# An encoder trunk's opening norm: one product spreads the sums, ScalarE seeds the inverse root, and a low part is issued ahead of a dot product

## The chip, the cores and the metric

The kernel runs on one core of a Trainium2 chip. The metric is the device time of one execution in microseconds (us), as the median of several runs. The core has a matrix engine (TensorE, "PE" in the profile, with its weight loads shown as "PEld"), a vector engine (VectorE, "DVE"), an activation engine (ScalarE, "ACT"), a general engine (GpSimd, "POOL") and a queue that issues most of the transfers (SyncE, "SP"). Each engine takes its instructions in the order in which they stand in its own program.

## The reference

Two layers, each made of a gated feed-forward half step, a mixer of three branches, and a second feed-forward half step. Every sub-layer starts with a norm that is shifted and scaled by values computed from a conditioning vector `c`. The change touches only the first norm of the first layer and what is multiplied with it:

```
def rms_norm(x, gain):
    xf = x.astype(jnp.float32)
    y = xf * lax.rsqrt(jnp.mean(xf * xf, axis=-1, keepdims=True) + EPS)
    return (y * gain.astype(jnp.float32)).astype(x.dtype)

def modulate(h, shift, scale):
    return h * (1 + scale[:, None, :]) + shift[:, None, :]

c_act = jax.nn.silu(c)
mod = (c_act @ w_ada[l] + b_ada[l]).reshape(B, N_MOD, D_MODEL)
h = modulate(rms_norm(x, norm_gain[l, 0]), mod[:, 0], mod[:, 1])
... swiglu(h, ffn_w_gate[l, 0], ffn_w_up[l, 0], ffn_w_down[l, 0])
```

There are 512 tokens of 1024 values. `mod[:, 0]` is the shift and `mod[:, 1]` the scale: 1024 values each, and each of them is a dot product of 1024 weights with `c_act`.

## The kernel before

**Layout.** Activations lie transposed: the 1024 features stand on 128 partitions in 8 blocks (`d` = 0 to 7), and the 512 tokens along the free axis. Every product is computed as three products: each operand is split into a high part in a narrower format and a low part (what the high part leaves over), and `triple` (lines 117 to 122) issues high x high, high x low and low x high. For a block of `h` these parts are `hhi` and `hlo`, for weights `whi` and `wlo`.

**The opening** is the method `start` of `Ffn`. x arrives in four transfers, ACT squares its eight blocks, and DVE adds the squares up (`ssum`, lines 693 and 695). The sum over the 128 partitions is made on PE: four products with one column of ones (line 699) give the sums of 4 x 128 tokens as a 128x4 tile. On that small tile DVE computes 1/sqrt with an integer first guess and three Newton steps (lines 299 to 308). To bring the result back along the free axis, DVE and ACT build four diagonal blocks (lines 708 and 710), and one product with a tile of ones (line 713) spreads them into `rb`, a 128x512 tile that holds 1/rms for every token on every partition.

**Then come the 8 blocks d.** For each one:

- two *dot products* on DVE (line 206, `mod_step`/`mod_dot`): the shift, written (0,d) below, and the scale, (1,d). Each reads a 128x1024 tile of `w_ada` that SP loads into one of four buffers with the tag "v2". The four are taken in turn, in the order (0,0), (1,0), (0,1), (1,1), ..., so that the load of a tile can be issued only when the dot product four places earlier in that order has been done;
- ACT makes the scale column `apre` from (1,d) (line 213);
- DVE multiplies x by `rb` (line 722, the tile `t`; two buffers);
- ACT writes `hhi` from `t` with scale and shift (line 724), and a second time in full precision into a PSUM tile (line 726);
- DVE writes `hlo` as the difference (line 727, "the low part");
- a 128x768 chunk of weights (`w_first`) is loaded into one of two raw buffers, ACT casts it to `whi`, GpSimd writes `wlo` (lines 290 and 292);
- PE issues 18 matmuls of 128x512 (3 gate and 3 up tiles, three products each).

**What sets the order.** A scheduler lays out the program of each engine. `tc.issue_after(x)` and `behind(engine)` only tell it that an instruction is to stand behind another one in the program. SP's transfers stand in the order (0,d), (1,d), chunk d, (0,d+1), and so on; a transfer that waits for its buffer holds up all that stand behind it. After the 8 blocks PE goes on with the gate and up products of the next weight tiles (`unit`, whose first weights are the pair `self.early`), and DVE with the remaining dot products (`mod_queue`), weight splits and block sums for later (line 490).

Of the kernel before, what the change touches and what calls it, by code (L numbers as in the profile page):

```python
# [15 lines left out]
F32 = mybir.dt.float32  # L16
F32R = mybir.dt.float32r
I32 = mybir.dt.int32
AF = mybir.ActivationFunctionType
ALU = mybir.AluOpType  # L20
AX = mybir.AxisListType

P = 128
T = 512
D = 1024
KD = D // P
# [5 lines left out]
NT = T // P  # L32
EPS = 1e-6
# [7 lines left out]
def encoder_kernel(tc, xT, c, w_ada, b_ada, gains, w_gate, w_up, w_down, w_qkv, w_f, w_ubg,  # L41
                   qk_gain, rel, fbias, w_pool, pool_scale, w_branch, w_out, inv_cnt, w_first, out):
    nc = tc.nc
    pools = []

    def open_pool(**kw):
        p = tc.tile_pool(**kw)
        pools.append(p)
        return p.__enter__()

    cp = open_pool(name="consts", bufs=1)
# [4 lines left out]
    mm = nc.tensor.matmul  # L56
# [3 lines left out]
    def nm(s):  # L60
        uid[0] += 1
        return f"{s}_{uid[0]}"

    def st(shape, dt, tag, bufs):
        return sb.tile(shape, dt, tag=tag, bufs=bufs, name=nm(tag))
# [4 lines left out]
    def mmt(shape=(P, T)):  # L70
        return ps.tile(list(shape), F32, tag="mm", bufs=4, name=nm("mm"))
# [5 lines left out]
    def t1(cols=T):  # L77
        return st([P, cols], F32, "t1", 2)

    def t2(cols=T):  # L80
        return st([P, cols], F32, "t2", 3)
# [52 lines left out]
    ident = cp.tile([P, P], F32, name="ident")  # L134
    make_identity(nc, ident)
    ones = cp.tile([P, P], F32, name="ones")
    nc.vector.memset(ones, 1.0)
    silc = [st([P, D], F32, "b", NB)]
    sil_dram = dr.tile([1, D], F32, name="sil_dram")
    crow = st([1, D], F32, "b", NB)  # L140
# [34 lines left out]
    hhi = cp.tile([P, KD, T], F32R, name="hhi")  # L175
    hlo = cp.tile([P, KD, T], F32R, name="hlo")
# [19 lines left out]
    def mod_step(l, j, d, tag="raw"):  # L196
        raw = st([P, D], F32, tag, {"v2": 4, "raw": NRAW, "b": NB}[tag])
        with after("dma"):
            nc.sync.dma_start(raw, w_ada[l, j, d])
        dot = lambda: mod_dot(raw, l, j, d)  # L200
        return dot() if in_start[0] else dot

    def mod_dot(raw, l, j, d):
        m = modc[:, l, j, d:d + 1]
        with after("norm"):
            dot = nc.vector.tensor_tensor_reduce(out=raw, in0=raw, in1=silc[0], scale=1.0,  # L206
                                                 scalar=badac[:, l, j, d:d + 1], op0=ALU.mult, op1=ALU.add,
                                                 accum_out=m).ins
        s, kind = divmod(j, 3)
        if kind == 1:  # L210
            g = gainc[:, l, s, d:d + 1]
            if in_start[0]:
                nc.scalar.activation(apre[:, l, s, d:d + 1], m, AF.Identity, scale=g, bias=g)
                return dot
            return nc.vector.scalar_tensor_tensor(apre[:, l, s, d:d + 1], m, 1.0, g, op0=ALU.add, op1=ALU.mult).ins
        if kind == 2:
            nc.vector.tensor_scalar(m, m, 0.5, None, op0=ALU.mult)

    mod_queue = [(l, j, d) for l in range(L) for j in range(9) for d in range(KD)][16:]
    mod_ptr = [0]  # L220
# [30 lines left out]
    gate = {}  # L251
    quiet = [0]

    @contextlib.contextmanager
    def behind(engine):

        if engine in gate:
            with tc.issue_after(gate[engine]):
                yield
        else:  # L260
            yield
# [50 lines left out]
    def rsqrt(v, n):  # L312
        return list(rsqrt_steps(v, n))[-1]

    def xd(d):
        return x_blocks[d // 2][:, d % 2, :]
# [258 lines left out]
    class Ffn:  # L575
# [112 lines left out]
        def start(self):  # L688

            l = self.l  # L690
            ssum = st([P, T], F32, "ssum", 1)
            tiles = [sq[:, a, :] for sq in squares for a in range(2)]
            fold = nc.vector.tensor_tensor(ssum, tiles[0], tiles[1], op=ALU.add)
            for tile_ in tiles[2:]:
                fold = nc.vector.tensor_tensor(ssum, ssum, tile_, op=ALU.add)
            gate["vector"] = fold.ins
            pv = mmt((P, NT))
            for t in range(NT):
                mm(pv[:, t:t + 1], ssum[:, t * P:(t + 1) * P], ones[:, 0:1], start=True, stop=True)
            with behind("vector"):  # L700
                mod_step(l, 0, 0, "v2")
            v = st([P, NT], F32, "nt_v4", 1)
            nc.vector.tensor_scalar(v, pv, 1.0 / D, EPS, op0=ALU.mult, op1=ALU.add)
            r = rsqrt(v, NT)
            dg = st([P, NT, P], F32, "ssum", 1)
            for t in range(NT):
                if t % 2:
                    nc.scalar.activation(dg[:, t, :], ident, AF.Copy, scale=r[:, t:t + 1])
                else:
                    gate["vector"] = nc.vector.tensor_scalar(dg[:, t, :], ident, r[:, t:t + 1], None, op0=ALU.mult).ins  # L710
            spread = gate["vector"]
            rb = mmt()
            mm(rb, ones, dg.rearrange("p a b -> p (a b)"), start=True, stop=True)
            pgs = [(acc(), acc()), (acc(), acc()), (mmt(), mmt())]

            with behind("vector"):
                ready = [mod_step(l, 1, 0, "v2")]
            gate.clear()

            def h(d):  # L720
                t = t1(T)
                scaled = nc.vector.tensor_tensor(t, rb, xd(d), op=ALU.mult).ins
                a, b = apre[:, l, 0, d:d + 1], modc[:, l, 0, d:d + 1]
                nc.scalar.activation(hhi[:, d, :], t, AF.Identity, scale=a, bias=b)  # L724
                tb = mmt()
                nc.scalar.activation(tb, t, AF.Identity, scale=a, bias=b)
                nc.vector.tensor_tensor(hlo[:, d, :], tb, hhi[:, d, :].bitcast(F32), op=ALU.subtract)  # L727
                if d + 1 < KD:
                    with tc.issue_after(ready[0]):
                        mod_step(l, 0, d + 1, "v2")  # L730
                    with tc.issue_after(scaled):
                        ready[0] = mod_step(l, 1, d + 1, "v2")

            def product(d, w):
                for n in range(3):
                    for which in range(2):
                        i = 3 * which + n
                        triple(pgs[n][which], w[0][:, i, :], w[1][:, i, :], hhi[:, d, :], hlo[:, d, :],
                               d == 0, d == KD - 1)

            for d in range(KD):
                if d == 0:
                    gate["vector"] = spread
                w = wchunk(w_first[d], (6, P), side=False, lo_eng=nc.gpsimd)
                gate.clear()
                h(d)
                product(d, w)
            in_start[0] = False
            self.early = self.gate_up(0, 3), self.gate_up(1, 3)
            late_inputs()  # L750
            return [self.act(n, *pgs[n]) for n in range(3)]
# [557 lines left out]
```

## Time and profile before

| | |
|---|---|
| median of 3 runs | 2392.25 us (2389.51 to 2394.1) |
| profiled execution | 2394.31 us, of which 2392.4 us is the span from the first to the last instruction |
| PE busy | 2357.9 us, 99% of the span |
| DVE busy | 1738.8 us, 73% |
| ACT busy | 1201.4 us, 50% |
| POOL busy | 315.9 us, 13% |
| granted TensorE clock | 1.0 (mean) |

A row of the timeline reads: start in us from the beginning of the span, duration in us, engine, line, operation, output <- input, shapes, count. In brackets stands the idle time of the engine just before it and what ended that idle time. Instructions that follow each other on one engine and line may be merged in one row ("x2", "x4"). In a row of windows the first figure is the length of the stretch, and the figure behind each engine is its busy time in it. On PE, the start of one matmul to the start of the next is the measure, since the ends are modelled. The opening takes the first 59 us; PE is continuously busy for the 41 us after that.

### The profile page before, as it was taken

The page shows a single profiled execution, that of the slowest core. Times are in us where ns is not written, and L with a number is a line of the kernel's source. Part 1 is how long each engine was busy: PE and PEld are TensorE (multiplying, and loading weights), DVE is VectorE, ACT ScalarE, POOL GpSimd, SP SyncE. Part 2 cuts the span into 40 slices and gives each one's busy share as a digit, 9 for nine tenths or more (in the row PEclk, how much of TensorE's full clock was granted, in tenths as well). Part 3 has the DMA queues.
Part 4 walks back from the last instruction along what each step waited for, and adds up shares of the span by engine and source line. Part 5 has one row for each costly group of instructions (what it writes and reads, how often), then busy time and mean ns, then how long its engine had stood idle before and what let it go on. Part 6 is the DMA issues. An engine that isn't in the chain of part 4 may idle for free.

```text
span 2392.4 us, 36842 instructions
## 1 busy us (share of the span) xinstructions
PE 2357.9 (99%) x14106; PEld 2086.4 (87%) x14106; DVE 1738.8 (73%) x3090; ACT 1201.4 (50%) x2090; POOL 315.9 (13%) x401
## 2 busy tenths in 40 slices
PE   7999999999999999999999999999999999999999
PEld 5898998778888898989998989978788888889898
DVE  8887866787685576878677878577866855768583
ACT  5353555786632353635553636466865324536252
POOL 3000011144312200000000000102443222000000
PEclk9999999999999999999999999999999999999999
DMA  7535342223355534353325353323233554223322
GB/s 284 203 106 185 105 143 80 94 80 109 119 199 200 193 106 151 115 178 105 133 80 194 101 190 106 135 84 100 78 117 111 220 202 158 99 96 106 104 96 102
DMA packets 116436, 320.93 MB, mean 134 GB/s; under 512 B 11138, under 2 KB 13314, under 8 KB 116260
## 3 DMA queue, kind: packets, MB, share of 16 engines
q1 hardware_dynamic: 115106, 314.38, 38.6%
q0 software_dynamic: 1152, 4.19, 0.4%
q8 instruction: 111, 1.82, 0.3%
q14 instruction: 65, 0.53, 0.1%
q10 hardware_dynamic: 2, 0.00, 0.0%
HBM read 312.16 MB, written 6.38 MB: 133 GB/s over the span
## 4 chain that ended last, share of the span: by engine, by line
PE 85%; DVE 7%; ACT 5%; issue 2%; DMA 1%; SPq 0%; DVEq 0%; ACTq 0%; POOL 0%; POOLq 0%
PE acc L119 15%; PE acc L120 15%; PE acc L121 15%; PE mm L119 4%; PE mm L120 4%; PE mm L121 4%; PE mm L129 4%; PE mm L128 4%; PE mm L130 4%; PE acc L128 4%; PE acc L129 4%; PE acc L130 4%; ACT b L859 1%; PE mm L997 1%; DVE v L206 1%
## 5 line engine op out<-in xcount | busy, mean ns | idle before, releaser
L290 ACT CAST whi<-raw 128x1024 fp32r<-128x1024 f32 (+1 forms) x267 | 277.4, 1043 | 438.3 <-PE acc L120 255.7
L292 DVE TENSOR_TENSOR wlo<-raw,whi 128x1024 fp32r<-128x1024 f32 x259 | 319.6, 1237 | 160.5 <-ACT whi L290 157.8
L119 PE MATMUL acc<-b,whi 128*128 128x512 f32 (+1 forms) x960 | 360.7, 376 | 0.0
L120 PE MATMUL acc<-b,whi 128*128 128x512 f32 (+1 forms) x960 | 357.0, 372 | 0.0
L121 PE MATMUL acc<-b,wlo 128*128 128x512 f32 (+1 forms) x960 | 356.6, 371 | 0.0
L119 PEld LDWEIGHTS acc<-b,whi 128*128 128x128 f32 x960 | 180.8, 188 | 31.7 <-DVE xv L447 0.3
L121 PEld LDWEIGHTS acc<-b,wlo 128*128 128x128 f32 x960 | 180.8, 188 | 31.5
L120 PEld LDWEIGHTS acc<-b,whi 128*128 128x128 f32 x960 | 180.9, 188 | 29.8
L119 PE MATMUL acc<-hhi,whi 128*128 128x512 f32 x480 | 191.1, 399 | 3.3 <-ACT hhi L724 1.7
L120 PE MATMUL acc<-hlo,whi 128*128 128x512 f32 x480 | 188.3, 392 | 1.4 <-DVE hlo L727 1.4
L121 PE MATMUL acc<-hhi,wlo 128*128 128x512 f32 x480 | 188.0, 392 | 0.0
L398 DVE TENSOR_TENSOR ptb<-v,ptb 128x1024 fp32r<-128x1024 f32 x128 | 156.6, 1224 | 35.8 <-ACT ptb L397 33.9
L397 ACT CAST ptb<-v 128x1024 fp32r<-128x1024 f32 x128 | 134.0, 1050 | 95.4 <-DVE v L465 54.6
L397 ACT CAST whi<-raw 128x1024 fp32r<-128x1024 f32 (+1 forms) x128 | 106.7, 834 | 99.2 <-PE acc L120 52.8
L119 PE MATMUL acc<-whi,hhi 128*128 128x512 f32 x336 | 137.8, 411 | 0.9 <-DVE xv L398 0.9
L121 PE MATMUL acc<-whi,hlo 128*128 128x512 f32 x336 | 131.9, 393 | 0.0
L120 PE MATMUL acc<-wlo,hhi 128*128 128x512 f32 x336 | 131.7, 392 | 0.0
L206 DVE CUSTOM_DVE_ANT_0 v<-v,b,badac 128x1024 f32<-128x1024 f32 x87 | 116.1, 1341 | 20.5 <-DMA v<-in_w_ada_dram 20.3
L398 DVE TENSOR_TENSOR wlo<-raw,whi 128x1024 fp32r<-128x1024 f32 (+1 forms) x128 | 122.0, 953 | 6.8 <-ACT whi L397 5.0
L447 DVE SCALAR_TENSOR_TENSOR xv<-acc,modc,xv 128x512 f32<-128x512 f32 (+1 forms) x112 | 77.3, 691 | 63.4 <-PE acc L121 63.4
L119 PEld LDWEIGHTS acc<-hhi,whi 128*128 128x128 f32 x480 | 90.7, 189 | 21.4 <-ACT hhi L724 3.3
L119 PE MATMUL mm<-hhi,whi 128*128 128x512 f32 x280 | 109.3, 391 | 0.0
(313 smaller groups left out, 6594.9 us busy)
## 6 DMA issues: line engine op xcount, KB each, us to landing
raw<-in_w_down_dram SPq DMA_DIRECT2D x88, 512.0 KB, 3.7
v<-in_w_ada_dram SPq DMA_DIRECT2D x87, 512.0 KB, 5.4
raw<-in_w_up_dram SPq DMA_DIRECT2D x82, 512.0 KB, 3.9
raw<-in_w_gate_dram SPq DMA_DIRECT2D x79, 512.0 KB, 3.6
b<-in_w_ada_dram SPq DMA_DIRECT2D x57, 512.0 KB, 5.2
raw<-in_w_ubg_dram SPq DMA_DIRECT2D x56, 512.0 KB, 3.5
raw<-in_w_qkv_dram SPq DMA_DIRECT2D x42, 512.0 KB, 3.6
raw<-in_w_branch_dram SPq DMA_DIRECT2D x24, 512.0 KB, 3.6
```

What stands on the lines that cost most here:

```text
L119: mm(o, lh, rh, start=start, stop=False)
L120: mm(o, lh, rl, start=False, stop=False)
L121: mm(o, ll, rh, start=False, stop=stop)
L128: mm(o, lh, rh, start=start and k == 0, stop=False, skip_group_check=True)
L129: mm(o, lh, rl, start=False, stop=False, skip_group_check=True)
L130: mm(o, ll, rh, start=False, stop=k == 3, skip_group_check=True)
L206: dot = nc.vector.tensor_tensor_reduce(out=raw, in0=raw, in1=silc[0], scale=1.0, scalar=badac[:, l, j, d:d + 1], op0=ALU.mult, op1=ALU.add ...
L290: nc.scalar.copy(hi, raw)
L292: lo_eng.tensor_tensor(lo, raw, hi.bitcast(F32), op=ALU.subtract)
L397: nc.scalar.copy(hi, src)
L398: nc.vector.tensor_tensor(lo, src, hi.bitcast(F32), op=ALU.subtract)
L447: nc.vector.scalar_tensor_tensor(x, acc_j, gate, x, op0=ALU.mult, op1=ALU.add)
```

## The change

1. The sum over partitions and its spread become one product: `ones` (128x128) times `ssum` (128x512) gives `total`, in which every partition holds every token's sum. The four small products, the diagonal blocks and the second product go.
2. 1/sqrt is computed on 128x512: ACT reads `total` with its function `Abs_reciprocal_sqrt` (`seed`; the epsilon comes from a new 128x1 tile) and squares the seed; DVE computes mean + epsilon (`var`) and one Newton step in two instructions, the second of which writes `rb` in PSUM. The function needs another table on ACT: the program has one table load ahead of it and one ahead of the first `Silu` that follows.
3. The first two dot products, (0,0) and (1,0), both stand ahead of this.
4. In each block, the order that is asked of DVE becomes: `t` of block d, dot product (0,d+1), low part `hlo` of d, dot product (1,d+1). Before, both dot products were tied to their predecessors and the low part was free.
5. The gate that placed GpSimd's first low part behind the diagonal blocks goes.

```diff
+    eps = cp.tile([P, 1], F32, name="eps")
+    nc.vector.memset(eps, EPS)
...
-            pv = mmt((P, NT))
-            for t in range(NT):
-                mm(pv[:, t:t + 1], ssum[:, t * P:(t + 1) * P], ones[:, 0:1], start=True, stop=True)
+            total = mmt()
+            mm(total, ones, ssum, start=True, stop=True)
             with behind("vector"):
                 mod_step(l, 0, 0, "v2")
-            v = st([P, NT], F32, "nt_v4", 1)
-            nc.vector.tensor_scalar(v, pv, 1.0 / D, EPS, op0=ALU.mult, op1=ALU.add)
-            r = rsqrt(v, NT)
-            dg = st([P, NT, P], F32, "ssum", 1)
-            for t in range(NT):
-                if t % 2:
-                    nc.scalar.activation(dg[:, t, :], ident, AF.Copy, scale=r[:, t:t + 1])
-                else:
-                    gate["vector"] = nc.vector.tensor_scalar(dg[:, t, :], ident, r[:, t:t + 1], None, op0=ALU.mult).ins
-            spread = gate["vector"]
+                mod_step(l, 1, 0, "v2")
+            seed, square = t2(T), t2(T)
+            nc.scalar.activation(seed, total, AF.Abs_reciprocal_sqrt, scale=1.0 / D, bias=eps)
+            gate["scalar"] = nc.scalar.activation(square, seed, AF.Square).ins
+            var = t1(T)
+            nc.vector.tensor_scalar(var, total, 1.0 / D, EPS, op0=ALU.mult, op1=ALU.add)
             rb = mmt()
-            mm(rb, ones, dg.rearrange("p a b -> p (a b)"), start=True, stop=True)
+            nc.vector.scalar_tensor_tensor(var, square, -0.5, var, op0=ALU.mult, op1=ALU.mult)
+            nc.vector.scalar_tensor_tensor(rb, var, 1.5, seed, op0=ALU.add, op1=ALU.mult)
             pgs = [(acc(), acc()), (acc(), acc()), (mmt(), mmt())]
-
-            with behind("vector"):
-                ready = [mod_step(l, 1, 0, "v2")]
-            gate.clear()
...
-                nc.vector.tensor_tensor(hlo[:, d, :], tb, hhi[:, d, :].bitcast(F32), op=ALU.subtract)
-                if d + 1 < KD:
-                    with tc.issue_after(ready[0]):
-                        mod_step(l, 0, d + 1, "v2")
-                    with tc.issue_after(scaled):
-                        ready[0] = mod_step(l, 1, d + 1, "v2")
+                low = lambda: nc.vector.tensor_tensor(hlo[:, d, :], tb, hhi[:, d, :].bitcast(F32), op=ALU.subtract).ins
+                if d + 1 == KD:
+                    low()
+                    return
+                with tc.issue_after(scaled):
+                    shift = mod_step(l, 0, d + 1, "v2")
+                with tc.issue_after(shift):
+                    done = low()
+                with tc.issue_after(done):
+                    mod_step(l, 1, d + 1, "v2")
...
             for d in range(KD):
-                if d == 0:
-                    gate["vector"] = spread
                 w = wchunk(w_first[d], (6, P), side=False, lo_eng=nc.gpsimd)
```

**DVE in the middle blocks.** In the rows, `t_..` is the tile `t`, `hlo` the low part, and the `v_..` of an ISA row is the `w_ada` tile of a dot product. Before, from the `t` of block 2 (the dot products are (0,3), (1,3), (0,4), (1,4), the low parts those of blocks 2 and 3):

```order
L722 TENSOR_TENSOR t_53_255<-mm_163,xv_85 128x512
L206 ISA v_55_261,modc<-v_55_261,b_73,badac 128x1024
...
L206 ISA v_56_264,modc<-v_56_264,b_73,badac 128x1024
...
L727 TENSOR_TENSOR hlo<-mm_258,hhi 128x512
L722 TENSOR_TENSOR t_60_292<-mm_163,xv_85 128x512
L206 ISA v_62_298,modc<-v_62_298,b_73,badac 128x1024
...
L722 TENSOR_TENSOR t_67_329<-mm_163,xv_92 128x512
L727 TENSOR_TENSOR hlo<-mm_295,hhi 128x512
L206 ISA v_63_301,modc<-v_63_301,b_73,badac 128x1024
```

And after the change, from the `t` of block 2 (the dot products are (0,3), (1,2), (0,4), (1,3), the low parts those of blocks 1 and 2):

```order
L717 TENSOR_TENSOR t_44_234<-mm_145,xv_87 128x512
L208 ISA v_46_239,modc<-v_46_239,b_75,badac 128x1024
...
L722 TENSOR_TENSOR hlo<-mm_200,hhi 128x512
L208 ISA v_40_206,modc<-v_40_206,b_75,badac 128x1024
...
L717 TENSOR_TENSOR t_51_271<-mm_145,xv_87 128x512
L208 ISA v_53_276,modc<-v_53_276,b_75,badac 128x1024
...
L722 TENSOR_TENSOR hlo<-mm_237,hhi 128x512
L208 ISA v_47_243,modc<-v_47_243,b_75,badac 128x1024
```

What moved: DVE took the dot products in the order of their buffers, and now takes (0,d+2) ahead of (1,d+1), one low part behind.

**SP at the same place**, after the change; the order of these transfers is the same as before (the tiles are (0,3), (1,3), chunk 3, (0,4), (1,4), chunk 4):

```order
L201 DMA v_46_239<-in_w_ada_dram 128x1024
L201 DMA v_47_243<-in_w_ada_dram 128x1024
L282 DMA raw_265<-in_w_first_dram 128x768
L201 DMA v_53_276<-in_w_ada_dram 128x1024
L201 DMA v_54_280<-in_w_ada_dram 128x1024
L282 DMA raw_302<-in_w_first_dram 128x768
```

Nothing moved here: the load of (0,4) still stands behind the loads of (1,3) and chunk 3, and the load of (1,3) still waits for the buffer of (1,1).

**DVE at the last low part.** Before (`v_109` is the block sum of line 490; the dot products are (0,7) at `v_83`, (1,7) at `v_84`, then the first one of the later queue):

```order
L206 ISA v_83_409,modc<-v_83_409,b_73,badac 128x1024
...
L727 TENSOR_TENSOR hlo<-mm_406,hhi 128x512
L206 ISA v_84_412,modc<-v_84_412,b_73,badac 128x1024
...
L490 TENSOR_TENSOR v_109_553<-hhi,hlo 128x1024
L206 ISA v_90_464,modc<-v_90_464,b_73,badac 128x1024
...
L727 TENSOR_TENSOR hlo<-mm_443,hhi 128x512
L292 TENSOR_TENSOR wlo_469<-raw_466,whi_468 128x1024
L217 TENSOR_SCALAR modc<-modc 128x1
L206 ISA v_94_474,modc<-v_94_474,b_73,badac 128x1024
```

After (`v_75` is (1,7), `v_81` and `v_85` the first two of the later queue):

```order
L493 TENSOR_TENSOR v_100_532<-hhi,hlo 128x1024
L208 ISA v_81_443,modc<-v_81_443,b_75,badac 128x1024
...
L722 TENSOR_TENSOR hlo<-mm_385,hhi 128x512
L208 ISA v_75_391,modc<-v_75_391,b_75,badac 128x1024
...
L295 TENSOR_TENSOR wlo_448<-raw_445,whi_447 128x1024
L219 TENSOR_SCALAR modc<-modc 128x1
L208 ISA v_85_453,modc<-v_85_453,b_75,badac 128x1024
...
L722 TENSOR_TENSOR hlo<-mm_422,hhi 128x512
```

What moved: a weight split of 128x1024 and one more dot product now stand ahead of the last low part. On PE, the six high x high products of a block now stand ahead of its first product with `hlo` (in blocks 1 to 7); before, the first product with `hlo` was the second of the 18.

1 line of the change is left out of this document (added).

## The prediction

> **What bounds the kernel now.** I read the table of windows first, then the timeline of the opening, then who waited for whom, and last the transfers. The windows, cut at PE's first real product, at the rise of its pace, and at the end of the opening:
>
> ```profile
> 0.00:21.80 21.80, 7.72 (x14) 3.44 (x14) 14.06 (x29) 11.38 (x19) 4.10 (x8) 1.00 0.75 281
> 21.80:27.10 5.30, 5.29 (x13) 4.01 (x13) 5.30 (x8) 3.26 (x5) 1.19 (x2) 1.00 0.88 316
> 27.10:59.20 32.10, 30.68 (x134) 24.73 (x133) 31.93 (x45) 19.22 (x29) 12.94 (x6) 1.00 0.80 280
> 59.20:100.00 40.80, 40.80 (x182) 33.78 (x181) 39.78 (x60) 16.67 (x21) 0.00 (x0) 1.00 0.68 233
> ```
>
> The busy columns are PE, PEld, DVE, ACT, POOL; the last three are clock, DMA share and GB/s. Until 21.8 us PE has nearly nothing to do. From 27.1 to 59.2 us PE and DVE are both full: two resources are nearly level. After 59.2 us PE never stops, so whatever the opening gains or loses at its end is carried to the end of the kernel.
>
> ```profile
> 11.60 1.86 PE L699 MATMUL mm<-ones,ssum 128*128 128x1 f32 x8 [4.14 <-DVE ssum L695]
> 13.79 1.80 POOL L292 TENSOR_TENSOR wlo<-raw,whi 128x768 fp32r<-128x768 f32 x1 [12.48 <-ACT whi L290]
> 13.91 1.70 DVE L306 TENSOR_TENSOR nt_q<-nt_j 128x4 f32<-128x4 f32 x1
> 18.05 2.07 PE L713 MATMUL mm<-ssum,ones 128*128 128x512 f32 x2 [4.58 <-ACT ssum L708]
> 20.16 0.69 DVE L722 TENSOR_TENSOR t<-mm,xv 128x512 f32<-128x512 f32 x1
> 20.95 0.81 ACT L724 ACTIVATE hhi<-t,modc,apre 128x512 fp32r<-128x512 f32 x1 [0.83 <-DVE t L722]
> 21.81 2.08 PE L119 MATMUL acc<-hhi,whi 128*128 128x512 f32 x4 [1.69 <-ACT hhi L724]
> 27.10 0.40 PE L120 MATMUL acc<-hlo,whi 128*128 128x512 f32 x1
> 41.51 0.50 PE L120 MATMUL acc<-hlo,whi 128*128 128x512 f32 x1 [0.38 <-DVE hlo L727]
> 55.09 0.50 PE L120 MATMUL acc<-hlo,whi 128*128 128x512 f32 x1 [1.04 <-DVE hlo L727]
> 58.64 0.39 PE L120 MATMUL mm<-hlo,whi 128*128 128x512 f32 x1
> 58.87 0.39 PE L121 MATMUL mm<-hhi,wlo 128*128 128x512 f32 x1
> PE acc L120 <- DVE hlo L727: 1.4, 2, 1.0
> ```
>
> The norm runs from the end of the sums (11.6) to the first `t` (20.16). Warm matmuls start 0.227 us apart, so a block of 18 costs PE 4.09 us. From 27.1 us PE stood only twice, before 41.51 and 55.09, each time for a low part. The last product starts at 58.87, so PE is free at 59.1.
>
> **The norm, part by part.** The product that replaces line 699 has the shape of line 713: 2.07 us, from 11.60 to 13.67. (1,0) moves into this wait. The seed on ACT lies between 0.60 us (`Silu` from PSUM) and 0.81 (line 724, with two column operands); it has one: 0.70, to 14.4.
>
> ```profile
> 1.28 1.28 ACT L142 ACT_TABLE_LOAD   x1 [1.28 <-PEq L1297]
> 2.58 1.05 ACT L142 ACTIVATE b<-b 1x1024 f32<-1x1024 f32 x1
> 10.17 1.05 ACT L157 COPY b<-mm 128x512 f32<-128x512 f32 x2
> 23.13 0.39 ACT L213 ACTIVATE apre<-modc,gainc 128x1 f32<-128x1 f32 x1 [0.70 <-DVE modc L206]
> 55.85 0.60 ACT L571 ACTIVATE t<-acc 128x512 f32<-128x512 f32 x1 [2.48 <-PE acc L121]
> 4.74 1.15 ACT L150 ACTIVATE whi<-xv 128x512 f32<-128x512 f32 x2 [1.11 <-DMA xv<-in_xT_dram]
> 101.43 0.75 DVE L447 SCALAR_TENSOR_TENSOR xv<-acc,modc,xv 128x512 f32<-128x512 f32 x1
> ```
>
> The table load stands behind the copies that end at 11.22. With 1.28 us it ends at 12.5, in the wait for the product: nothing. The second load stands ahead of the first `Silu`, where ACT was idle for 2.48 us: nothing.
>
> By the Trainium skill (ScalarE: Activation LUTs, What ACT_TABLE_LOAD costs) a switch costs 1.28 us and a drain of about 1.38, 2.66 in all. The row above shows its activation 1.30 us after the load's start; by the page the seed would start at 13.9 instead of 13.7, and the sum below would be 0.2 us larger.
>
> Then `apre` (0.39) and the square (half of 1.15) on ACT, to 15.35; `var` lies beside them. The two Newton instructions cost 0.70 each (a three-operand op of this width took 0.75, `t` 0.69): 16.75. `t` 0.69, `hhi` 0.81 and the hand-overs: PE starts at 18.4, 3.4 us earlier than now.
>
> **A lock shared by GpSimd and DVE.** The 1.70 us of line 306 above (0.16 elsewhere) ends with the POOL row beside it. The same later:
>
> ```profile
> 26.02 1.27 DVE L206 CUSTOM_DVE_ANT_0 v<-v,b,badac 128x1024 f32<-128x1024 f32 x1
> 26.11 2.88 POOL L292 TENSOR_TENSOR wlo<-raw,whi 128x768 fp32r<-128x768 f32 x1 [4.11 <-DVE hlo L727]
> 27.22 0.68 DVE L722 TENSOR_TENSOR t<-mm,xv 128x512 f32<-128x512 f32 x1
> 27.82 2.26 DVE L206 CUSTOM_DVE_ANT_0 v<-v,b,badac 128x1024 f32<-128x1024 f32 x1
> 30.01 0.08 DVE L206 DVE_READ_ACCUMULATOR2_ANT modc<- 128x1 f32 x1
> ```
>
> POOL, normally 1.8 us, took 2.88: it began work when the dot product ended (27.22) and ran to 28.99. The next dot product then ended 1.02 us behind POOL. `t`, with an input in PSUM, ran through. So a dot product takes 1.20 us (start to next start), `t` and `hlo` 0.60, and a dot product that meets a POOL op up to 1.2 more.
>
> In the new norm the first POOL op is ready at 16.15 (cast of 0.83 behind the square), and so is the second Newton instruction: a tie. If DVE is first, POOL runs from 16.85 to 18.6 and holds (0,1) until 19.6; (1,1), held by the second POOL op in the same way, ends at 22.8. If POOL is first, `rb` is 1.6 us later and (1,1) ends at 24.4. Before, it ended at 23.02:
>
> ```profile
> 20.77 2.32 DVE L206 CUSTOM_DVE_ANT_0 v<-v,b,badac 128x1024 f32<-128x1024 f32 x1
> 23.02 0.08 DVE L206 DVE_READ_ACCUMULATOR2_ANT modc<- 128x1 f32 x1
> ```
>
> I take the middle, 23.6, and keep both. PE's early start is thus not DVE's: the dot products start no earlier.
>
> **The new order of DVE against the order of the loads.** Before, dot products ran in the order of their buffers, and the waits on `w_ada` tiles in the first 80 us came to 0.8 us. Now (0,d+3) runs ahead of (1,d+2), but its load still stands on SP behind that of (1,d+2), which waits for the buffer of (1,d). So (1,d) must end; then SP issues (1,d+2), chunk d+2, (0,d+3); then (0,d+3) must land; then (0,d+3), `hlo` of d+1, (1,d+2) run on DVE. That is a ring over two blocks.
>
> ```profile
> 30.11 1.53 SPq L199 DMA_DIRECT2D v<-in_w_ada_dram  x2
> 38.30 0.37 SPq L279 DMA_DIRECT2D raw<-in_w_first_dram  x1
> 39.68 1.53 SPq L199 DMA_DIRECT2D v<-in_w_ada_dram  x2
> v<-in_w_ada_dram SPq DMA_DIRECT2D x1, 512.0 KB, 5.6
> DMA to landing us min/median/max: 4.9/5.3/7.5
> DVE v L206 <- DMA v<-in_w_ada_dram: 0.8, 1, 0.8
> ```
>
> The first row confirms the rule: the load at 30.11 follows the dot product that ended at 30.01, by 0.1. The fourth is the load at 39.68, which went out 1.4 us behind a chunk and took 5.6 us. In the new ring the load goes out 0.4 us behind the chunk; if the queue sets the pace it waits 1.0 longer, 6.6; the spread seen is 4.9 to 7.5. I take 6.1. The way to the landing is 0.1 + 2 x 0.37 (two issues) + 6.1 = 7.0 us. Behind it come 1.2 + 0.6 + 1.2 on DVE, and 1.2 for a POOL op, whose chunk lands just ahead and whose cast is done when the dot product starts. The ring takes 11.2 us; PE needs 8.2 for the same two blocks.
>
> Three rounds lead from (1,1) over (1,3) and (1,5) to (1,7): 33.6 us, and the block sum (line 490, now in the last round) adds 1.1. (1,7) ends at 23.6 + 34.7 = 58.3.
>
> **The last block.** The weight split and one more dot product now stand ahead of the last low part:
>
> ```profile
> 54.35 0.68 DVE L727 TENSOR_TENSOR hlo<-mm,hhi 128x512 fp32r<-128x512 f32 x1
> 54.96 1.21 DVE L292 TENSOR_TENSOR wlo<-raw,whi 128x1024 fp32r<-128x1024 f32 x1
> 56.15 1.27 DVE L206 CUSTOM_DVE_ANT_0 v<-v,b,badac 128x1024 f32<-128x1024 f32 x1
> ```
>
> That is 1.13 + 1.2 + 0.67 = 3.0, so the low part is ready at 61.3 (now 55.0). ACT's way from (1,7) to it (0.42 + 0.72 + 0.76) lies beside. The regrouping on PE leaves 12 products behind it instead of 17: 2.75 us. PE is free at 64.05.
>
> **The sum.** 64.05 - 59.1 = +4.95 us. Behind the opening PE is full, and nothing is late that it wants: the extra split and dot product were done early, so DVE is about 3 us late and PE about 5. The profiled execution would go from 2394.31 to 2399.3; it lies 2.06 above the median, so the median of runs goes to 2397.2. A measurement of this kernel can tell about 0.2%, 4.8 us.
>
> **Rivals.**
>
> 1. *PE leads, the loads keep up.* If the ring takes 8.2 us or less, PE sets the pace: it starts 3.4 us earlier and its two stops (0.52 and 1.19) may go too: -3.4, at most -5.1. The time is 2388.9, at best 2387.2. For it: PE and DVE are level now, and DVE gave up the small-tile chain. It decides when the third load lands within 5.2 us of (1,d)'s end and meets no POOL op (5.2 + 3.0 = 8.2), or within 4.0 with one. Against it: the quickest `w_ada` load took 4.9 from its own issue, 5.7 with the issues ahead of it.
> 2. *The ring is partly covered.* Loads at 5.3 (6.2 with the issues) and a POOL op that hits only every other round: 9.8 a round, 4.2 less in all: +0.7, 2393.
> 3. *Worse than the ring.* Landings at the 7.5 end and POOL ahead in the tie: 3 x 1.4 + 0.8 = 5.0 more: +10, 2402.2. The DMA share of 0.80 to 0.88 leaves room for this, since the ring's three loads are issued in a bunch.
>
> **How the numbers follow.** The forecast case is +2.5 to +8.5 (2394.7 to 2400.7 is its own range): 0.68, with 0.47 of it above 4.8. Rival 1: 0.12, half of it beyond -4.8, where both stops go. Rival 2: 0.08. Rival 3: 0.12. So faster 0.06, same 0.06 + 0.08 + 0.21 = 0.35, slower 0.47 + 0.12 = 0.59. The range from 2389.5 to 2402 leaves out most of rival 1 and half of rival 3.
>
> **What the profile after would show.** PE's first product near 18.4 (20.0 if POOL wins the tie). Idle time of DVE ahead of the dot products (0,4) to (0,7), released by `w_ada` transfers: some 1 to 3 us a round, where only 0.8 stands now. PE waiting for `hhi` or `hlo` in nearly every block, with starts of blocks some 5.6 us apart. The last low part near 61, the last opening product near 64, and from there the same distances as before. The prediction is wrong if the `w_ada` waits stay under 1 us in all, or if PE, late by 5 us at 64, is not late by 5 us at the end.

## The result and the profile after

The changed kernel takes 2397.38 us (median of 12 runs, 2396.36 to 2400.44), the kernel before, run beside it, 2391.23 us (12 runs, 2389.51 to 2394.61). The ratio is 1.0027, with a 95% interval of 1.0019 to 1.0034: slower by 6.15 us, where 4.95 were forecast. The time came out almost as forecast. The reason given for it did not hold: most of the 6 us is lost far behind the opening, by something that the prediction does not mention. The profiled execution after took 2396.62 us, with a span of 2394.7.

The windows of the changed kernel, cut at PE's first real product, at the same 27.10 as before, and where PE is free of the opening (columns as before):

```profile
0.00:18.45 18.45, 5.85 (x6) 1.66 (x6) 11.17 (x18) 12.24 (x19) 3.02 (x7) 1.00 0.87 332
18.45:27.10 8.65, 8.37 (x27) 6.00 (x28) 8.65 (x13) 3.98 (x6) 4.03 (x2) 1.00 0.68 232
27.10:60.90 33.80, 29.09 (x121) 21.75 (x120) 31.52 (x44) 20.27 (x29) 11.39 (x6) 1.00 0.84 276
60.90:100.00 39.10, 39.10 (x174) 32.40 (x173) 36.86 (x54) 17.32 (x22) 0.00 (x0) 1.00 0.66 214
```

PE starts at 18.45 and is free at 60.9, 1.8 us later than the 59.1 of before, and not 64.05. In the third window PE has lost its fullness (29.1 of 33.8 us), while DVE keeps nearly all of it (31.5).

The timeline of the new norm:

```profile
11.35 1.28 ACT L706 ACT_TABLE_LOAD   x1
11.70 2.08 PE L701 MATMUL mm<-ssum,ones 128*128 128x512 f32 x2 [3.78 <-DVE ssum L698]
13.81 0.69 ACT L706 ACTIVATE t<-mm,eps 128x512 f32<-128x512 f32 x1 [1.18 <-PE mm L701]
15.34 0.69 DVE L711 SCALAR_TENSOR_TENSOR t<-t,t 128x512 f32<-128x512 f32 x1
16.06 0.70 DVE L712 SCALAR_TENSOR_TENSOR mm<-t,t 128x512 f32<-128x512 f32 x1
16.10 2.33 POOL L295 TENSOR_TENSOR wlo<-raw,whi 128x768 fp32r<-128x768 f32 x1 [14.79 <-DVE t L711]
17.41 2.10 DVE L208 CUSTOM_DVE_ANT_0 v<-v,b,badac 128x1024 f32<-128x1024 f32 x1
18.45 2.08 PE L119 MATMUL acc<-hhi,whi 128*128 128x512 f32 x4 [4.68 <-ACT hhi L719]
20.64 2.16 DVE L208 CUSTOM_DVE_ANT_0 v<-v,b,badac 128x1024 f32<-128x1024 f32 x1
```

Product, seed, two Newton instructions of 0.7 us, first product at 18.45: all as forecast. The tie at 16.1 went to DVE by 0.04 us. The dot products (0,1) and (1,1), which meet a POOL op each, take 2.1 and 2.16 us; (1,1) ends at 22.7.

DVE and PE farther on in the opening, from the timeline and the table of waits (18 to 66 us):

```profile
29.71 1.66 DVE L208 CUSTOM_DVE_ANT_0 v<-v,b,badac 128x1024 f32<-128x1024 f32 x1 [0.50 <-DMA v<-in_w_ada_dram]
40.17 2.50 DVE L208 CUSTOM_DVE_ANT_0 v<-v,b,badac 128x1024 f32<-128x1024 f32 x1 [1.77 <-DMA v<-in_w_ada_dram]
53.59 1.27 DVE L208 CUSTOM_DVE_ANT_0 v<-v,b,badac 128x1024 f32<-128x1024 f32 x1
57.20 0.68 DVE L722 TENSOR_TENSOR hlo<-mm,hhi 128x512 fp32r<-128x512 f32 x1
58.17 0.39 PE L120 MATMUL acc<-hlo,whi 128*128 128x512 f32 x1
60.66 0.39 PE L121 MATMUL mm<-hhi,wlo 128*128 128x512 f32 x1
DVE v L208 <- DMA v<-in_w_ada_dram: 2.3, 2, 1.8
PE acc L120 <- DVE hlo L722: 3.3, 6, 1.4
```

Two dot products, (0,4) and (0,6), wait for their loads, 2.3 us in all. But (1,7), at 53.59, ends at 54.8 and not at 58.3, and the last low part starts at 57.20 and not at 60.6 (ready 61.3).

Nor are the links of the ring those of the prediction. SP's issues (SPq) and the ends of dot products on DVE, in the changed kernel:

```profile
24.05 2.13 SPq L201 DMA_DIRECT2D v<-in_w_ada_dram  x2
25.75 0.07 DVE L208 DVE_READ_ACCUMULATOR2_ANT modc<- 128x1 f32 x1
28.53 0.08 DVE L208 DVE_READ_ACCUMULATOR2_ANT modc<- 128x1 f32 x1
31.84 0.37 SPq L282 DMA_DIRECT2D raw<-in_w_first_dram  x1
33.11 0.08 DVE L208 DVE_READ_ACCUMULATOR2_ANT modc<- 128x1 f32 x1
33.21 3.13 SPq L201 DMA_DIRECT2D v<-in_w_ada_dram  x2
```

The first row holds the loads of (0,4) and (1,4). The second of them went out at 25.85, 0.1 us behind the end of (0,3) (second row); the buffer that would have been its turn is that of (1,2), which ended only at 28.53. So the four buffers are no longer taken in turn: from (1,4) on, a load takes the buffer that DVE frees next. The load of (0,6) thus follows the end of (1,3) at once (33.11 and 33.21). It does not stand behind a load that waits for (1,3): that of (1,5) and chunk 5 (31.84) had gone out before.

Now a place of which the prediction says only that nothing is late there. Lines 128 to 130 (`add_product`) issue products of 256 columns, 5,376 of them in eight stretches of 672. Here the fifth stretch, of the kernel before (its second profile, the control below). A row gives the durations in ns (least, median, largest) and the first and the last start in us; the stretch goes from the first start of the second row to the last start of the third:

```profile
L128 PE MATMUL mm<-b,ptb x48: 277/280/285, 1319.7 to 1383.5; 128*128 128x256 f32 x48
L128 PE MATMUL acc<-hhi,whi x32: 277/283/283, 1306.9 to 1369.3; 128*128 128x256 f32 x32
L130 PE MATMUL mm<-b,wlo x16: 281/282/283, 1325.7 to 1386.6; 128*128 128x256 f32 x16
```

And the same stretch of the changed kernel:

```profile
L128 PE MATMUL mm<-b,ptb x48: 283/283/283, 1321.9 to 1386.3; 128*128 128x256 f32 x48
L128 PE MATMUL acc<-hhi,whi x32: 277/283/283, 1308.9 to 1371.9; 128*128 128x256 f32 x32
L130 PE MATMUL mm<-b,wlo x16: 283/283/283, 1327.9 to 1389.4; 128*128 128x256 f32 x16
```

Before, the stretch lasts 79.7 us (1306.9 to 1386.6), after, 80.5 (1308.9 to 1389.4). From the starts in the trace it is 79.71 and 80.51 us, or 118.8 and 120.0 ns from product to product. Nobody waits in this stretch, the clock is 1.0 in both, and the instructions are the same. Eight stretches make 8 x 0.80 = 6.4 us; added up from the two traces, the eight take 638.05 and 644.1 us.

### The profile page after: what moved, and what is told of

It reads as the page before. It is cut to its first block, busy times and chain, and to the rows that moved or that the text cites. A ratio compares the mean times of both kernels' runs of the same rounds, so it can differ in the third digit from the quotient of the medians.

```text
span 2394.7 us, 36815 instructions
## 1 busy us (share of the span) xinstructions
PE 2361.2 (99%) x14098; PEld 2090.0 (87%) x14098; DVE 1738.0 (73%) x3081; ACT 1204.8 (50%) x2092; POOL 316.4 (13%) x401
## 4 chain that ended last, share of the span: by engine, by line
PE 88%; DVE 5%; ACT 5%; issue 1%; DMA 1%; SPq 0%; DVEq 0%; ACTq 0%
PE acc L119 15%; PE acc L121 15%; PE acc L120 15%; PE mm L130 4%; PE mm L129 4%; PE mm L128 4%; PE acc L130 4%; PE acc L129 4%; PE acc L128 4%; PE mm L120 4%; PE mm L121 4%; PE mm L119 4%; ACT b L856 1%; PE mm L994 1%; ACT b L859 1%
## 5 line engine op out<-in xcount | busy, mean ns | idle before, releaser
L120 PEld LDWEIGHTS acc<-hlo,whi 128*128 128x128 f32 x480 | 90.7, 189 | 22.4 <-DVE hlo L722 6.6
```

The costliest lines, as they stand in the source:

```text
L120: mm(o, lh, rl, start=False, stop=False)
```

## The experiments

All were timed in five rounds beside the kernel before. The first three take the change apart, and the fourth is a control.

**The new norm alone**, with the old order of dot products and low parts:

```diff
 (against the changed kernel)
-                mod_step(l, 1, 0, "v2")
+                ready = [mod_step(l, 1, 0, "v2")]
...
-                low = lambda: nc.vector.tensor_tensor(hlo[:, d, :], tb, hhi[:, d, :].bitcast(F32), op=ALU.subtract).ins
-                if d + 1 == KD:
-                    low()
-                    return
-                with tc.issue_after(scaled):
-                    shift = mod_step(l, 0, d + 1, "v2")
-                with tc.issue_after(shift):
-                    done = low()
-                with tc.issue_after(done):
-                    mod_step(l, 1, d + 1, "v2")
+                nc.vector.tensor_tensor(hlo[:, d, :], tb, hhi[:, d, :].bitcast(F32), op=ALU.subtract)
+                if d + 1 < KD:
+                    with tc.issue_after(ready[0]):
+                        mod_step(l, 0, d + 1, "v2")
+                    with tc.issue_after(scaled):
+                        ready[0] = mod_step(l, 1, d + 1, "v2")
```

> The new norm (one product, seed on ScalarE, one Newton step, (1,0) ahead of it) with the order of dot products and low parts as before the change. Theory 'ring' (the loss is that dot product (0,d+3) needs a load that stands behind the load that waits for (1,d)): the dot products run in buffer order again, so the waits for w_ada in the first 60 us fall from 2.3 us to under 0.5 us, and the last opening product ends within 1 us of 59.1 us; the time is within 2 us of before. Rival 'norm' (the loss comes from the new norm itself, its table load or its meeting with GpSimd): the time stays 4 to 7 us above before.

Measured: 2396.25 us, ratio 1.0022 (1.0013 to 1.0030). The shortest of the eight stretches takes 80.51 us, as in the changed kernel. The time is that of the rival "norm"; the theory "ring" wanted at most 2 us more than before.

**The new order alone**, with the old norm (the lines with - and + above the other way round, in the kernel before):

> The new order of dot products and low parts with the old norm (small tile, diagonal blocks). Theory 'ring': the loss is there without the new norm, and larger, since the norm's earlier start is missing: waits for w_ada of 2 us or more in the first 60 us, last opening product at 61 to 64 us, time 5 to 9 us above before. Rival 'norm': within 2 us of before.

Measured: 2398.06 us, ratio 1.0025 (1.0015 to 1.0036). The shortest stretch takes 79.71 us, as before. Here the theory "ring" is met and the rival "norm" is not. Two halves of the change that each cost 5 to 7 us, and together 6: they cannot be the same 6 us.

**The changed kernel with loads that wait for no dot product.** The `w_ada` tiles of blocks 2 to 7 go into buffers of their own; the order of DVE, ACT, PE and SP stays.

```diff
-                    low()
+                    gate["vector"] = low()
...
-                    shift = mod_step(l, 0, d + 1, "v2")
+                    shift = mod_step(l, 0, d + 1, "b" if d else "v2")
...
-                    mod_step(l, 1, d + 1, "v2")
+                    mod_step(l, 1, d + 1, "b" if d else "v2")
...
-            late_inputs()
+            tail = gate.pop("vector")
+            with tc.issue_after(tail):
+                late_inputs()
```

> The changed kernel, with the w_ada tiles of blocks 2 to 7 in buffers of the tag b, of which 15 are free here, so that no load of them waits for a dot product; order of instructions on DVE, ACT, PE and SP as in the changed kernel. Theory 'ring': no dot product waits for w_ada in the opening beyond 0.5 us; the last low part comes 2 to 4 us earlier than the changed kernel's 57.2; the time falls by 2 to 5 us against the changed kernel, to at most 2 us above before (what stays is the last low part behind a weight split and one more dot product, and GpSimd's lock). Rival 'lock and last block alone' (the ring costs nothing): the time stays within 1 us of the changed kernel, 5 to 7 us above before.

Measured: 2397.03 us, ratio 1.0023 (1.0014 to 1.0033). No dot product waits for a load any more in the opening, and the first 256-column product starts at 124.6 us, where the changed kernel had 125.9. So the waits for loads cost 1.3 us in this pair of profiles, and the time, which fell by 0.35 us where the theory "ring" wanted 2 to 5, is not made by them. In this run (1,1) ends at 22.5 and (1,7) at 53.5: without any wait for loads DVE itself takes 30.9 us for these three rounds.

**The kernel before, once more**, as a control:

> The kernel before, unchanged, profiled a second time and timed against itself, since the two profiled executions differ by 2.3 us where the medians differ by 6.2. If the shown profile of before was one of its slow executions, this one's span is 2 to 4 us shorter than 2392.4 and one stage shows where; if the difference arises only in unprofiled runs, its span is again within 1 us of 2392.4. Ratio 1.000 with an interval of about 0.001 to either side.

Measured: 2391.49 us, ratio 0.9999 (0.9991 to 1.0008). Its first 256-column product starts at 125.0; the first profile of before had 124.4. A single profile's opening is thus known to some 0.6 us. Its span is 2389.4 us, 3.0 less than that of the first profile of before, and the eight stretches show where: they take 5.0 us more in the first profile. There PE waited in some of them for a copy of a finished sum by ScalarE (line 559):

```profile
PE mm L128 <- ACT v L559: 1.7, 3, 1.2
PE acc L128 <- ACT v L559: 1.3, 3, 0.4
```

In the control and in the changed kernel no such wait is listed. These waits come and go from one execution of the same kernel to the next, so the shortest of the eight stretches is the one to compare.

What the slow stretches have in common (the first and the third run, and the changed kernel) is the new norm, which does not run any more at 1300 us. What remains of it there is where the tiles lie. A tile's place in a partition follows from the sizes of all tiles allotted before it, in the order of first use. The tile `eps` takes 32 bytes, so `hhi`, `hlo`, `b`, `whi`, `wlo` and `v2` move up by 0x20; the small tiles of the old norm are no longer allotted ahead of `ptb`, so `ptb` moves down by 0x300. From `b` (first buffer at 0xcc00) to `ptb` (0x30f20) it was 0x24320 bytes, and is now 0x24000 (0xcc20, 0x30c20). Theories A to D stand in the first expectation of the next four.

**The kernel before with the unused tile `eps`:**

```diff
     nc.vector.memset(ones, 1.0)
+    eps = cp.tile([P, 1], F32, name="eps")
+    nc.vector.memset(eps, EPS)
```

> The kernel before, with the tile eps (32 bytes of each partition) and its memset put behind ones as in the changed kernel; nothing reads it. Every tile allocated later lies 32 bytes higher: hhi, hlo, b, whi, wlo and v2 now 32 past a multiple of 64 (before: at one), ptb at a multiple of 64 (before: 32 past one). Theory A (a 256-column product is faster where the left tile and the right tile differ in their place within 64 bytes; in the changed kernel ptb and b are alike): they still differ, so 118.8 ns from product to product as before and 2391 us. Theory B (what counts is that b and hhi start on a multiple of 64): 120.0 ns, 5,368 intervals x 1.2 ns = 6.4 us more, 2397 us. Theory C (the distance of ptb from the others, 0x300 smaller in the changed kernel) and theory D (not the addresses but the instructions of the new norm): 118.8 ns and 2391 us.

Measured: 2392.01 us, ratio 1.0003 (0.9994 to 1.0012), shortest stretch 79.71 us. It is not the place of `b` and `hhi` by itself: B falls.

**The kernel before with `ptb` moved by 32 unused bytes:**

```diff
+            st([P, 8], F32, "pad", 1)
             v = st([P, NT], F32, "nt_v4", 1)
```

> The kernel before, with 32 bytes of each partition left unused ahead of nt_v4, so that raw, t1, t2 and ptb lie 32 bytes higher; not one instruction is added. b, hhi and whi stay on a multiple of 64, and ptb is now on one too. Theory A (alike is slow): 120.0 ns from product to product and 2397 us. Theory B (b and hhi on a multiple of 64 are fast), C (the distance of ptb, smaller by 0x300) and D (the new norm's instructions): 118.8 ns and 2391 us.

Measured: 2390.70 us, ratio 0.9996 (0.9988 to 1.0005), shortest stretch 79.65 us. All these tiles are on a multiple of 64, and it is fast: A falls too, in the form it was put.

**The changed kernel with the places of before, to 64 bytes:**

```diff
-    eps = cp.tile([P, 1], F32, name="eps")
+    eps = cp.tile([P, 16], F32, name="eps")[:, 0:1]
...
+            st([P, 8], F32, "pad", 1)
             seed, square = t2(T), t2(T)
```

> The changed kernel, with eps as 64 bytes instead of 32 and 32 unused bytes ahead of t2: hhi, hlo, b, whi, wlo and v2 on a multiple of 64 and ptb 32 past one, as in the kernel before; the instructions are those of the changed kernel. Theories A and B: 118.8 ns from product to product, and of the change only what it does to the opening is left, 0.9 to 1.6 us: 2392 to 2393 us. Theory C (the distance of ptb stays 0x300 smaller) and D (the new norm's instructions): 120.0 ns and 2397 us.

Measured: 2390.31 us, ratio 0.9999 (0.9990 to 1.0008). With every instruction of the change, but other places, the loss is gone. C (the smaller distance is kept) and D (the instructions are kept) fall. Two rows of line 128 in this run, the first of the whole run, the second of the fifth stretch:

```profile
L128 PE MATMUL acc<-hhi,whi x256: 277/283/284, 124.5 to 2321.1; 128*128 128x256 f32 x128
L128 PE MATMUL mm<-b,ptb x48: 277/280/286, 1317.1 to 1380.9; 128*128 128x256 f32 x48
```

The first row's first start, 124.5, ends the opening: no later than before. The products with `ptb` are back at a median of 280 instead of 283 ns.

**The kernel before with `whi`, `wlo` and `v2` moved by 32 bytes, `ptb` by 64:**

```diff
         xb = blk("xv", F32)
+        if b == 0:
+            st([P, 8], F32, "pad1", 1)
...
+            st([P, 8], F32, "pad", 1)
             v = st([P, NT], F32, "nt_v4", 1)
```

> The kernel before, with 32 unused bytes ahead of whi and 32 ahead of nt_v4, and no instruction added: b, hhi and hlo on a multiple of 64, whi, wlo, v2, raw and ptb 32 past one. Theory A: the products of hhi and hlo with whi and wlo, alike before and at 120.0 ns, fall to about 118.8 as well: some 1,470 intervals x 1.2 ns = 1.8 us less, 2389.4 us, and more if the 512-column products (203.9 ns in every kernel so far) gain too. Theories B, C and D: nothing changes, 2391 us.

Measured: 2417.05 us (only four runs), ratio 1.0111 (1.0097 to 1.0124). None of the theories had this. The stretches are the fastest of all (79.57 us), since the products of `hhi` with `whi` now gain as well. But products of 512 columns lose. From the whole run, line 120 of before:

```profile
L120 PE MATMUL acc<-b,whi x960: 278/389/398, 92.0 to 2388.6; 128*128 128x512 f32 x160, 128*128 128x256 f32 x32
```

and of this run, with a row of the 256-column products:

```profile
L120 PE MATMUL acc<-b,whi x960: 277/395/397, 92.7 to 2410.9; 128*128 128x512 f32 x160, 128*128 128x256 f32 x32
L128 PE MATMUL acc<-hhi,whi x256: 277/281/286, 126.1 to 2347.9; 128*128 128x256 f32 x128
```

389 ns became 395. Over some 7,040 intervals from product to product in lines 119 to 121 the mean rises from 203.9 to 207.9 ns: 28 us, of which the faster stretches give 1.1 back; 25.4 were measured, and the difference is not placed.

So I formed theory E: what counts is the distance between the tiles of the left and the right operand, modulo some power of two above 64. At zero, 256-column products are slow and 512-column products fast; elsewhere the other way round. In the changed kernel `ptb` has come to zero (0x24000). `hhi` and `whi`, 0x1d300 apart, had 120.0 ns all along; if that counts as zero too, the period is 128 or 256. The last four runs test this.

**The changed kernel with 64 unused bytes ahead of `t2`** (distance 0x40):

```diff
+            st([P, 16], F32, "pad", 1)
             seed, square = t2(T), t2(T)
```

> The changed kernel with 64 unused bytes of each partition ahead of t2, no instruction added: ptb now lies 0x40 past b and whi, counted modulo 256, where the changed kernel has 0; it is still 32 past a multiple of 64, as they all are. Theory E (what counts is the distance of the left operand's tile from the right one's, modulo 128 or 256: at zero a 256-column product takes 120.0 ns, else 117 to 119): pace 118.7 ns as with the same distance in the kernel before, 5,368 x 1.3 = 7 us less than the changed kernel: 2390 to 2391 us. Theory F (slow where every tile is 32 past a multiple of 64): 120.0 ns and 2397 us.

Measured: 2390.43 us, ratio 0.9997 (0.9988 to 1.0005), shortest stretch 79.66 us.

**The kernel before, with its old norm, brought to distance zero:**

```diff
+    eps = cp.tile([P, 1], F32, name="eps")
+    nc.vector.memset(eps, EPS)
...
-            v = st([P, NT], F32, "nt_v4", 1)
+            v = t2(T)[:, :NT]
```

> The kernel before, its old norm and its old order, with eps and its memset put behind ones (nothing reads it) and v of the norm in a buffer of t2 instead of a tile of its own: b, hhi and whi move up by 32 bytes and ptb stays, so that ptb is at distance zero from them modulo 256, as in the changed kernel. Theory E: 120.0 ns from product to product, 6.4 us more than the kernel before: 2397 to 2398 us, with an opening as before. Theory D (the new norm's instructions slow the products): 118.8 ns and 2391 us.

Measured: 2397.72 us, ratio 1.0026 (1.0016 to 1.0036). This is the loss of the change without the change:

```profile
L128 PE MATMUL mm<-b,ptb x48: 283/283/283, 1321.3 to 1385.7; 128*128 128x256 f32 x48
L128 PE MATMUL acc<-hhi,whi x32: 278/283/283, 1308.3 to 1371.3; 128*128 128x256 f32 x32
L130 PE MATMUL mm<-b,wlo x16: 283/283/283, 1327.3 to 1388.8; 128*128 128x256 f32 x16
```

The stretch takes 80.5 us, and the opening ended as before (first 256-column product at 124.4 us).

**The changed kernel at distance 0x80:**

```diff
+            st([P, 1], F32, "mx", 4)
             seed, square = t2(T), t2(T)
```

> The changed kernel with the four small buffers of mx allotted ahead of t2 instead of behind, no instruction added: ptb lies 0x80 past b and whi modulo 256. If theory E holds with a period of 128 bytes: 120.0 ns and 2397 us, as the changed kernel. With a period of 256 bytes: 117 to 119 ns and 2390 to 2392 us.

Measured: 2393.96 us, ratio 1.0009 (1.0000 to 1.0017), shortest stretch 79.92 us: between the two, nearer to the fast end. The time lies outside both forecasts (2397, and 2390 to 2392). At 0x80 the products are not as slow as at zero, so the period is not 128, and 256 fits all runs; but half of it is not as good as a quarter. Distances from 0xa0 on were not tried for these products.

**The new norm with the old order, at distance 0x40** (the first run, with the 64 unused bytes of the run that brought the changed kernel to 0x40):

> The new norm with the old order of dots and low parts (the run named e1_norm_only), and ptb moved on by 64 unused bytes. Theory E: 118.7 ns a product, 7 us less than the 2396.25 us of that run: 2389.3 us, so that the norm alone would be 2 us faster than the kernel before. By its opening, which ended 2.2 to 2.9 us later than that of the two profiles of before, it should rather come to 2393 us. Theory D: 120.0 ns and 2396 us.

Measured: 2391.07 us, ratio 0.9996 (0.9988 to 1.0005): 5.2 us less than the same kernel at distance zero. That lies between the two forecasts (2389.3 by the time, 2393 by the opening): the opening of the run at distance zero had been late by an accident of its own, with the sums ready 1.6 us later (13.0 against 11.3) and the granted clock at 0.5 from 34.05 to 37.46 us, and here it ended at 124.2 (there at 127.3). The norm alone thus gains nothing that can be told, though it is shorter. The timeline of this run shows why:

```profile
14.84 1.28 DVE L208 CUSTOM_DVE_ANT_0 v<-v,b,badac 128x1024 f32<-128x1024 f32 x1
15.79 4.20 POOL L295 TENSOR_TENSOR wlo<-raw,whi 128x768 fp32r<-128x768 f32 x2 [14.48 <-ACT whi L293]
16.04 2.29 DVE L712 SCALAR_TENSOR_TENSOR t<-t,t 128x512 f32<-128x512 f32 x1
18.36 2.18 DVE L713 SCALAR_TENSOR_TENSOR mm<-t,t 128x512 f32<-128x512 f32 x1
22.23 2.08 PE L119 MATMUL acc<-hhi,whi 128*128 128x512 f32 x4 [8.76 <-ACT hhi L720]
```

In the old order a third dot product stands ahead of the Newton step. POOL begins 0.25 us ahead of DVE, and each Newton instruction takes 2.2 to 2.3 us instead of 0.7. PE starts at 22.23, and not at 18.45.

All runs side by side (distances in bytes of a partition, modulo 256; the stretch is the shortest of the eight):

| kernel | `b` to `ptb` | `hhi` to `whi` | stretch, us | median, us |
|---|---|---|---|---|
| before (control) | 0x20 | 0 | 79.71 | 2391.49 |
| before, eps unused | 0x20 | 0 | 79.71 | 2392.01 |
| before, `ptb` moved | 0x40 | 0 | 79.65 | 2390.70 |
| before, `whi` moved | 0x60 | 0x20 | 79.57 | 2417.05 |
| before, alike | 0 | 0 | 80.51 | 2397.72 |
| order alone | 0x20 | 0 | 79.71 | 2398.06 |
| norm alone | 0 | 0 | 80.51 | 2396.25 |
| norm alone, 64 on | 0x40 | 0 | 79.65 | 2391.07 |
| changed | 0 | 0 | 80.51 | 2397.38 |
| changed, free loads | 0 | 0 | 80.51 | 2397.03 |
| changed, places of before | 0x20 | 0 | 79.71 | 2390.31 |
| changed, 64 on | 0x40 | 0 | 79.66 | 2390.43 |
| changed, 128 on | 0x80 | 0 | 79.92 | 2393.96 |

With 64 unused bytes the changed kernel is 7 us faster than without them, and level with the kernel before; no version here is measurably faster than the kernel before.

## Why the prediction was right, and where it was wrong

The time (2397.2 forecast, 2397.38 measured) and the sign were right. The sum behind them was wrong: the opening lost far less than forecast, and a loss that the prediction put at nothing came behind it. That the two errors nearly cancelled is luck.

- **The norm** was right: first product at 18.45 (forecast 18.4), the tie for DVE, (1,1) at 22.7 (22.8 by the better of the two ends, 23.6 taken). The table load was hidden: the seed started at 13.81, 0.03 us behind the end of the product. By the Trainium skill (ScalarE: Activation LUTs, What ACT_TABLE_LOAD costs) it would have stood 2.66 us behind the load's start, at 14.0; the trace shows 2.46, so that the whole drain was not seen here. It was not seen at the second load either: that began at 57.80, and the `Silu` behind it at 59.10, 1.30 us later. The idle time of ScalarE that was to hide this second load was not there, but no product of PE waited for it.
- **The ring** was mis-sized, and its links were partly others. From (1,1) to (1,7) the forecast was 33.6 + 1.1 = 34.7 us; it took 32.1, in rounds of 10.4, 11.3 and 10.4. Two of the three rounds waited for a load, 2.3 us in all, where 1 to 3 a round were forecast. In these two, the way from the end of (1,1) or (1,3) to the start of the dot product that waited took 6.98 and 7.06 us, with 7.0 forecast. In the second round this is luck: the load went out at once, and took longer than forecast. What was too large is the rest: in the first round GpSimd held the dot product for 0.4 us and not 1.2, and in the third no load was waited for, and DVE's own work, the block sum included, was all there was (10.4 us instead of 12.3). The comparison of 11.2 us with PE's 8.2 misled, too: DVE's own work in three rounds, the block sum and what POOL holds up included, is 30.9 us, as the run with free loads shows. The waits for loads add 1.2 us to that, not the 9 (3 x 3.0) that lie between the ring and PE. I took PE for what it would hold up, where DVE was already the slower one.
- **The last block** was right: 3.0 us from the end of (1,7) to the ready low part (54.8 to 57.8), 0.35 more until PE took it, 12 products behind it in 2.7 us.
- **The opening's sum** then is +1.8 us in this pair of profiles (60.9 for 59.1), not +4.95: 0.9 less by the tie and 2.6 less by the ring, and 0.35 more at the last low part. Over five profiles with the old norm and order (the run with `whi` moved is left out, since its 512-column products are slower) the first 256-column product starts at 124.2 to 125.0 us (mean 124.5). Over the four with both halves of the change, which differ only in the places of their tiles, it starts at 124.5 to 125.9 (mean 125.1). That is +0.6 us, close to rival 2 (the ring partly covered, +0.7), but profiles that scatter by 0.8 and 1.5 us do not tell it from nothing, and with other places the changed kernel's time (2390.3 and 2390.4 us) shows no loss. The two halves do pull against each other, as the expectation of the order alone said: with the order alone that product starts at 128.9, +4.4, and the early start of the norm takes nearly all of it back. Of the 6.9 us that the order alone costs in time I can place these 4.4. Its profile has 4.6 us more in the eight stretches than the control's, where PE waits for the same copies by ScalarE (2.6 us in all); but the first profile of before has 5.0 more too, so that the rest stays open.
- **"Behind the opening PE is full, and nothing is late that it wants"** is the step on which the time was lost. PE is full and nothing is late, but its 256-column products take 1.2 ns more each on average, by a 32-byte tile and the changed order of first use: 6.4 us by the shortest stretches, 6.05 by all eight of the control and the changed kernel. The test named there (PE late by 5 us at 64 and by 5 us at the end) fails: PE was late by 1.8 us at 61, or by 0.9 against the control at its first 256-column product, and by 5.3 against the control at the end. The eight stretches add 6.05 us in between, and some 1.6 come back elsewhere.

By the Trainium skill (SBUF — State Buffer, SBUF: two separate sides) only VectorE and GpSimd contend for a port, and TensorE waits for no one. The runs agree on the first (0.7 us became 2.3 beside a POOL op). On the second, they add that TensorE's pace depends on where its two operands lie to each other. Whether this is its weight load against its read of the moving operand, the runs do not show.

## What to carry to other kernels

A change that allots or drops a tile moves every tile behind it. Before a small difference in time is put down to the instructions, compare the durations of instructions that the change does not touch; if they differ evenly, restore the places with unused bytes and measure again. When a new wait is priced, compare it with the engine that already sets the pace there, not with the one that is hoped to.

## What the runs showed of the hardware that I had not expected

- From start to start (means over the eight stretches; the few intervals above 200 ns are left out), products of 128x128 by 128x256 (`b` with `ptb`) follow each other at 120.0 ns when the two tiles lie a multiple of 256 bytes apart, and at 118.3 ns at 0x20 more, 117.8 at 0x40, 118.9 at 0x60 and 118.6 at 0x80. `hhi` with `whi` went from 120.0 at zero to 118.5 at 0x20. One pair does not fit wholly: `b` with `whi` lies at zero in all kernels but one, and takes 120.0 in the changed kernel and with `ptb` at 0x40, but 119.0 to 119.3 with `ptb` at 0x20. Why is open.
- Products of 512 columns have it the other way round: 227 ns (median from start to start) at a multiple of 256, 233 to 234 at 0x20. This cost 25 us in one run, with 64 unused bytes and not one instruction changed.
- Two Newton instructions that met POOL's work took 2.29 and 2.18 us instead of 0.69 and 0.70. Which engine came first was decided by 0.04 us in the changed kernel and by 0.25 in the run with the norm alone, and PE's first product came 3.8 us later in the second, 3.1 of it by these two instructions.
